# Hybrid decoder layer on one Trainium2 core: additions and low parts of the norms from GpSimd to VectorE, and the sample's retention matmuls placed later

## The chip, the cores and the metric

The kernel runs on one core of a Trainium2 chip. The metric is the time of one execution in microseconds, measured on the device. The kernel before takes 2187.86 us, the median of three runs (2186.29 to 2188.22).

## What is computed

One step of a decoder layer for two groups of requests that share the weights: a prompt of 1024 tokens and a sample of 8 single tokens with their caches, 1032 columns in all. D_MODEL is 1024 and D_FF 2816, ALPHA the fourth root of 2. Cut to what matters here:

```
def layer_norm(x, g, b):
    mu = x.mean(-1, keepdims=True)
    var = jnp.square(x - mu).mean(-1, keepdims=True)
    return (x - mu) * lax.rsqrt(var + LN_EPS) * g + b

h = layer_norm(ALPHA * h + 0.5 * swiglu(h, up1, down1))
h = layer_norm(ALPHA * h + merge_branches(attn, ret, ...) )
h = layer_norm(ALPHA * h + 0.5 * swiglu(h, up2, down2))

# retention of the sample, per head, one token per request:
s_new = gamma * s_old + k (outer) v
o     = q @ s_new
```

The outputs are the layer's rows for both groups, the last 128 keys and values, and the retention states.

## The kernel before

**Layout.** Activations stand transposed: features on the 128 partitions, tokens along the row. Feature group d (0 to 7) of the residual is `Y(d, ...)`, kept in the tiles `ya` (d below 4) and `yb`. All 1032 columns are worked in three chunks of 384, 384 and 264 (`CH`). Each large product is made of three in a reduced format: a value x is kept as a high part and a low part (x less the high part), and TensorE adds high by high, high by low and low by high. The activations' parts stand in tiles `T` (`HH` and `HL` in the code).

**Weights.** Each 128x512 block of weights comes from memory into `raw`, a ring of four, over SP's queue of DMAs (L470). ScalarE writes its high part `w_hi`; VectorE subtracts that from `raw` and writes `w_lo`. VectorE therefore has a steady stream of `w_lo` operations in its queue in all stages.

**Stages.** FFN 1, norm 1 (`ln` with `li` 0), the combined projection with banded attention and retention beside it, the two gated output products, norm 2 (`ln` with `li` 1 for chunks 0 and 1, `ln_last` for chunk 2), FFN 2, norm 3 (`ln3`), and the output.

**What sets the order.** All engines run their queues in order, and the program writes one stream by hand with the class `Emit`. It keeps an estimated clock of TensorE (`E.pe`, which grows with each matmul) and an estimated free time of ScalarE, VectorE and GpSimd (`E.eng`). The helpers `E.mm`, `E.tr`, `E.act`, `E.tt`, `E.stt`, `E.ts`, `E.dve` and `E.ptt` emit one instruction and return its estimated end; `E.tt` and `E.stt` go to VectorE, `E.ptt` to GpSimd. The side work (norms, attention, retention) is written as generators. `yield t` means that a generator is taken up again at the first gap between two groups of matmuls where `E.pe` has reached t. So an estimate decides which matmuls of the main stream stand ahead of a generator's next matmul, and a different estimate moves everything that is emitted after it. Since the helpers record every operation at their own line, all TensorE matmuls have line L99, transposes L107, ScalarE L117, VectorE L121 and GpSimd's `tensor_tensor` L137; `rsqrt` runs on GpSimd at L753. Rows are told apart by their tiles.

**Banks.** The results of the main stream's units rotate through four PSUM banks (`mb`); a unit needs the evacuation of the unit four before it. Side work takes other banks from a pool (`sbanks`; the profile shows them as `sb` or `mb`).

**Norm 1 and 2, `ln`.** With a bank of the mean, VectorE subtracts it from the eight feature groups, ScalarE squares each difference into `lQ` or `lsq`, and seven additions gather the squares in `lQ`. A matmul with `onesm` makes the variance of it (L99, `onesm,ln`), GpSimd the inverse root, and another matmul spreads it over the partitions. Then VectorE multiplies each group by that and the gain; ScalarE adds the bias and, in norm 1, writes the high part to `HH`; the low part goes to `HL`. Norm 1 does this for d in `POOLD` (1, 4, 6) with one more operation on ScalarE, which adds the bias in place, and a subtraction on GpSimd; for the others VectorE does it in one `scalar_tensor_tensor`. The sums of y that the mean is made of are GpSimd's work as well (tile `ln` from `ln` and `ya` or `yb`), outside the diff.

**Norm 3, `ln3`.** The columns are transposed to rows of tokens, copied to `zt` by ScalarE, and VectorE takes the statistics. For chunks 0 and 1, six pieces of 128x512 each are scaled by ScalarE, multiplied by the gain on VectorE, added to the bias on GpSimd and stored.

**The sample's retention, `sret_gen`.** Eight units: half a head's states each, in two buffers `Sb` that take turns. For a unit GpSimd scales the state by gamma, four operations of VectorE add the outer product (`Sb` from `vB,so,Sb`), and one matmul with 128x512 (L99, `Sb,so`) reads the new state. Behind the matmul, SP's queue gets the store of the state (L1329) and the fetch of the state two units later into the same buffer (L1308, L1309), so that fetch waits for the store. The weight loads that the main stream needs stand in the same queue behind them.

Of the kernel before, what the change touches and what calls it, by code (L numbers as in the profile page):

```python
# [15 lines left out]
ALU = mybir.AluOpType  # L16
# [35 lines left out]
FETCH = 2.0  # L52
QUEUE = 8.0
SHORT = 1.3
POOLD = (1, 4, 6)
AHEAD = 0.5


# [170 lines left out]
def build(tc, I, O):  # L229
    nc = tc.nc  # L230
    E = Emit(nc)
    ctx = ExitStack()
    with ctx:
# [310 lines left out]
        def ln(c, li, t):  # L544
            n0, N = CH[c]
            W = LNW[c]
            nb = N // W
            while lnlock[0] is not None:
                yield 0.0
            lnlock[0] = c  # L550
            S = env["lS"][c % 2]
            lQ, lsq = env["lQ"], env["lsq"]
            yield t
            b1 = yield from sbanks.get()
            E.mm(b1[:, :N], onesm, S[:, :N], True, True)
            ts_ = {}
            for d in range(KD + 2):
                if d < KD:
                    yd = Y(d, n0, n0 + N)
                    t1 = E.tt(yd, yd, b1[:, :N], ALU.subtract, n=N)  # L560
                    q = lQ if d == 0 else lsq[d % 3]
                    ts_[d] = E.act(q[:, :N], yd, AF.Square, n=N, after=t1)
                e = d - 2
                if e > 0:
                    q = lsq[e % 3]
                    t = (E.ptt if e % 2 else E.tt)(lQ[:, :N], lQ[:, :N], q[:, :N], ALU.add, n=N, after=ts_[e])
                if d % 2 and d < KD:
                    yield E.pace(AHEAD) if li else E.pe + 0.9
            sbanks.put(b1, t1)
            yield t + 2.0 * li  # L570
            b2 = yield from sbanks.get()
            for i in range(nb):
                E.mm(b2[:W, i * P:(i + 1) * P], lQ[:, i * W:(i + 1) * W], onesm, True, True)
            t = E.ts(lv[:W, 0, :nb], b2[:W, 0:nb * P:P], LN_EPS, ALU.add, n=3)
            sbanks.put(b2, t)
            yield rsqrt(lv[:W, 0, :nb], lv[:W, 1, :nb], t)
            b3 = yield from sbanks.get()
            for i in range(nb):
                E.mm(b3[:, i * W:(i + 1) * W], lv[:W, 1, i:i + 1].to_broadcast([W, P]), ident[:W, :W], True, True)
            ts_ = {}  # L580
            for d in range(KD + 2):
                if d < KD:
                    yd = Y(d, n0, n0 + N)
                    t1 = E.stt(yd, yd, lnp[:, 2 * li, d:d + 1], b3[:, :N], ALU.mult, ALU.mult, n=N)
                    bd = lnp[:, 2 * li + 1, d:d + 1]
                    if li == 1:
                        t = E.act(yd, yd, AF.Identity, bias=bd, n=N, ptr=1, after=t1)
                    else:
                        t = E.act(HH(d, n0, N), yd, AF.Identity, bias=bd, n=N, ptr=1, after=t1)
                        if d in POOLD:  # L590
                            t = E.act(yd, yd, AF.Identity, bias=bd, n=N, ptr=1, after=t1)
                    ts_[d] = t
                e = d - 2
                if e >= 0 and li == 0:
                    ye = Y(e, n0, n0 + N)
                    he, le = f(HH(e, n0, N)), HL(e, n0, N)
                    if e in POOLD:
                        E.ptt(le, ye, he, ALU.subtract, n=N, after=ts_[e])
                    else:
                        t = E.stt(le, ye, lnp[:, 2 * li + 1, e:e + 1], he, ALU.add, ALU.subtract, n=N, after=ts_[e])  # L600
                if d % 2 and d < KD - 1:
                    yield E.pace(AHEAD) if li else E.pe + 0.9
            if li == 1:
                ds(out=hres[:, :, n0:n0 + N], in_=env["ya"][:, :, n0:n0 + N])
            sbanks.put(b3, t1)
            lnlock[0] = None
# [53 lines left out]
        def ln3(c):  # L660
# [5 lines left out]
            lQ, lsq = env["lQ"], env["lsq"]  # L666
# [12 lines left out]
            for pi, ds_ in enumerate(pieces):  # L679
# [4 lines left out]
                n = len(ds_) * P  # L684
# [29 lines left out]
            def norm(k):  # L714
                return E.act(zs[k], zs[k], AF.Identity, scale=r[:, k // 2:k // 2 + 1], bias=nm[:, k // 2:k // 2 + 1], n=512, ptr=2)

            if not smp:
                yield t
                E.stt(nm, mv[:, :, 0], -1.0, r, ALU.mult, ALU.mult, n=3)
                for k in ks:  # L720
                    t = E.tt(zs[k], zs[k], Gs[k], ALU.mult, n=512, after=norm(k))
                    E.ptt(zs[k], zs[k], Bs[k], ALU.add, n=512, after=t)
                    out(k)
                    yield E.pe + 1.0
                return
# [574 lines left out]
        def sret_gen():  # L1300
# [12 lines left out]
            t = E.act(v32, b[:32, 0:P], n=128)  # L1313
# [5 lines left out]
            for u in range(2 * RH):  # L1319
                h, hf = u // 2, u % 2  # L1320
                S, V = Sb[u % 2], vB[u % 2]
                t = E.pscale(S, S, GAMMA[h], n=512)
                yield t
                for i in range(4):
                    t = E.stt(S[:, i, :], V[:, i, :], so[:, 0, h, 4 * hf + i:4 * hf + i + 1], S[:, i, :], ALU.mult, ALU.add, n=128)
                yield t
                b = yield from sbanks.get()
                E.mm(b[:8, :], so[:, 1, h, :], S.rearrange("p b e -> p (b e)"), True, True)
                ds(out=O["ss"][h, :, 4 * hf:4 * hf + 4, :], in_=S)  # L1329
                if u + 2 < 2 * RH:  # L1330
                    fetch(u + 2)
                for i in range(4):
                    ii = 4 * hf + i
                    src = b[:8, i * P:(i + 1) * P]
                    if ii == 0:
                        t = E.ts(o8, src, i8[:, ii:ii + 1], ALU.mult, n=128)
                    else:
                        t = E.stt(o8, src, i8[:, ii:ii + 1], o8, ALU.mult, ALU.add, n=190)
                sbanks.put(b, t)
                if not hf:  # L1340
                    yield E.pe + 2.0
                    continue
                E.dve("bn_stats", 128, out=bn8[:, 0:6], in_=o8)
                E.dve("bn_aggr", 13, out=bn8[:, 6:8], in_=bn8[:, 0:6])
                t = rsqrt(bn8[:, 8:9], bn8[:, 9:10], E.ts(bn8[:, 8:9], bn8[:, 7:8], GN_EPS, ALU.add, n=1))
                yield t
                t = E.ts(zp, o8, bn8[:, 6:7], ALU.subtract, bn8[:, 9:10], ALU.mult, n=128)
                yield t
                b = yield from sbanks.get()
                E.tr(b[:, 0:8], zp, ident[:8, :8])  # L1350
                t = E.stt(Y(4 + h, NP, T), b[:, 0:8], 0.5, so[:, 3, h, :], ALU.mult, ALU.mult, n=8)
                sbanks.put(b, t)
                yield E.pe + 2.0
# [631 lines left out]
```

## Time and profile before

| what | value |
|---|---|
| median of three runs | 2187.86 us |
| the profiled execution | 2186.94 us |
| its span | 2185.2 us |
| TensorE busy | 2124.8 us, 97% |
| VectorE busy | 1486.8 us, 68% |
| ScalarE busy | 836.4 us, 38% |
| GpSimd busy | 201.3 us, 9% |
| mean granted clock of TensorE | 0.992 |

Busy times are those of the engine's own instructions. PE is TensorE, PEld its weight loads, DVE VectorE, ACT ScalarE, POOL GpSimd, SP the engine that issues the DMAs. A row of a timeline gives the start in us from the span's start, the duration of the row, the engine and line, the operation, the tile that is written, the tiles that are read, and how many like instructions the row joins; in brackets stands the idle time of the engine ahead of it and what released it. A row of a table of stretches gives the length and then the busy time of each engine with its number of instructions, the granted clock, and the DMAs' share. All times come from one execution under the profiler.

### The profile page before, as it was taken

The numbers are of one execution on the slowest core, as the hardware profiler recorded it, in microseconds if no ns is written. First come the engines' busy times: TensorE is split into PE (matmuls) and PEld (weight loads), VectorE is DVE, ScalarE is ACT, GpSimd is POOL, SyncE is SP. The second block draws the span as 40 slices with busy tenths as digits, with TensorE's granted clock in tenths as the row PEclk, the third lists the DMA queues.
The fourth block names the chain that finished last, engine by engine and source line by source line (L and its number), as shares of the span: only waits on it lengthen the run. The fifth ranks groups of instructions, "written<-read, shape, count | busy, mean of one in ns | idle before, by whom it ended". The sixth has DMA issues, their size and how long they took to land.

```text
span 2185.2 us, 39568 instructions
## 1 busy us (share of the span) xinstructions
PE 2124.8 (97%) x15865; PEld 2089.1 (96%) x15865; DVE 1486.8 (68%) x2699; ACT 836.4 (38%) x1585; POOL 201.3 (9%) x235
## 2 busy tenths in 40 slices
PE   8999999999999999999999999998999999999996
PEld 8999999999999889999979999997999999999996
DVE  7766666676866885566666747787767666576757
ACT  5333333342433674111324434544333333342323
POOL 1000000000005343111110201010000000000004
PEclk9999999999999999999999999999999999999998
DMA  4333333272630120111253434531323323364332
GB/s 141 119 100 115 117 104 111 99 295 66 235 128 28 48 61 21 41 41 41 90 182 129 138 125 135 184 123 58 118 97 127 107 98 127 105 263 167 135 98 78
DMA packets 116314, 250.85 MB, mean 115 GB/s; under 512 B 14242, under 2 KB 18178, under 8 KB 112274
## 3 DMA queue, kind: packets, MB, share of 16 engines
q1 hardware_dynamic: 115778, 248.27, 32.8%
q8 instruction: 125, 2.05, 0.4%
q14 instruction: 59, 0.48, 0.1%
q0 software_dynamic: 352, 0.05, 0.1%
HBM read 195.01 MB, written 54.29 MB: 114 GB/s over the span
## 4 chain that ended last, share of the span: by engine, by line
PE 82%; DVE 9%; DMA 4%; ACT 2%; issue 2%; POOL 1%; SPq 0%; DVEq 0%; ACTq 0%; POOLq 0%
PE pr L99 54%; PE mb L99 26%; DMA raw<-in_w_dram 3%; PE sb L99 1%; DVE T L121 1%; DVE ya L121 1%; DVE yb L121 1%; DVE w_lo L121 1%; DVE ln L121 1%; DVE zt L121 1%; ACT w_hi L117 1%; DMA adr<-ya 1%; PE sb L107 1%; DVE st L121 0%; ACT T L117 0%
## 5 line engine op out<-in xcount | busy, mean ns | idle before, releaser
L99 PE MATMUL pr<-T,w_hi 128*128 128x258 f32 x7008 | 1139.5, 285 | 22.1 <-DVE yb L121 5.6
L99 PEld LDWEIGHTS pr<-T,w_hi 128*128 128x128 f32 x7008 | 973.8, 191 | 27.3 <-ACT w_hi L117 8.3
L99 PE MATMUL pr<-T,w_lo 128*128 128x258 f32 x3504 | 710.4, 284 | 1.0 <-DVE w_lo L121 1.0
L99 PEld LDWEIGHTS pr<-T,w_lo 128*128 128x128 f32 x3504 | 548.1, 191 | 1.4 <-DVE w_lo L121 1.4
L99 PE MATMUL mb<-T,w_hi 128*128 128x384 f32 (+1 forms) x2208 | 526.7, 325 | 1.8 <-DVE yb L121 1.8
L121 DVE TENSOR_TENSOR w_lo<-raw,w_hi 128x512 fp32r<-128x512 f32 x500 | 355.8, 730 | 128.8 <-ACT w_hi L117 127.9
L117 ACT ACTIVATE w_hi<-raw 128x512 fp32r<-128x512 f32 x500 | 304.7, 625 | 272.4 <-PE pr L99 147.1
L99 PEld LDWEIGHTS mb<-T,w_hi 128*128 128x128 f32 x2208 | 378.6, 189 | 9.3 <-issue 5.5
L99 PE MATMUL mb<-T,w_lo 128*128 128x384 f32 (+1 forms) x1104 | 353.7, 320 | 0.0
L99 PEld LDWEIGHTS mb<-T,w_lo 128*128 128x128 f32 x1104 | 207.9, 188 | 0.0
L117 ACT ACTIVATE w_hi<-st 128x512 fp32r<-128x512 f32 x174 | 108.3, 630 | 187.2 <-DVE st L121 103.6
L121 DVE TENSOR_TENSOR a<-pr,a 128x516 f32<-128x516 f32 x87 | 60.5, 696 | 89.1 <-PE pr L99 85.4
L121 DVE TENSOR_TENSOR w_lo<-st,w_hi 128x512 fp32r<-128x512 f32 x174 | 115.4, 683 | 5.0 <-ACT w_hi L117 5.0
L117 ACT ACTIVATE a<-pr 128x516 f32<-128x516 f32 x86 | 51.5, 600 | 100.1 <-PE pr L99 97.5
L121 DVE SCALAR_TENSOR_TENSOR yb<-pr,yb 128x516 f32<-128x516 f32 x72 | 49.9, 694 | 54.0 <-PE pr L99 54.0
L121 DVE SCALAR_TENSOR_TENSOR ya<-pr,ya 128x516 f32<-128x516 f32 x72 | 49.9, 693 | 54.0 <-PE pr L99 53.9
L137 POOL TENSOR_TENSOR ln<-ya 128x384 f32<-128x384 f32 (+1 forms) x6 | 6.8, 1127 | 776.2 <-DVE ya L121 776.1
L117 ACT ACTIVATE th<-a 128x516 f32<-128x516 f32 x43 | 27.3, 635 | 126.0 <-DVE a L121 126.0
L121 DVE TENSOR_TENSOR T<-T 128x1032 fp32r<-128x1032 f32 (+1 forms) x72 | 70.5, 986 | 0.3 <-ACT T L117 0.3
L117 ACT ACTIVATE T<-T 128x1032 fp32r<-128x1032 f32 (+1 forms) x72 | 59.6, 863 | 18.2 <-DMA T<-tdr 17.1
L753 POOL TENSOR_TENSOR ln<-ln,mhalf 128x3 f32<-128x3 f32 (+2 forms) x4 | 3.5, 870 | 675.1 <-DVE ln L121 675.1
L121 DVE SCALAR_TENSOR_TENSOR gt<-gt,mb 128x384 f32<-128x384 f32 (+1 forms) x48 | 24.4, 509 | 60.6 <-PE mb L99 58.9
(320 smaller groups left out, 2288.6 us busy)
## 6 DMA issues: line engine op xcount, KB each, us to landing
raw<-in_w_dram SPq DMA_DIRECT2D x500, 256.0 KB, 2.9
T<-tdr SPq DMA_DIRECT2D x20, 1032.0 KB, 11.3
tdr<-ya SPq DMA_DIRECT2D x72, 258.0 KB, 2.6
T<-tdr SPq DMA_DIRECT2D x8, 2064.0 KB, 11.4
tdr<-s SPq DMA_DIRECT2D x40, 258.0 KB, 2.4
tdr<-m SPq DMA_DIRECT2D x32, 258.0 KB, 2.5
T<-adr SPq DMA_DIRECT2D x16, 516.0 KB, 4.7
out_yp_dram<-zt SPq DMA_DIRECT2D x16, 256.0 KB, 2.0
```

Of the source, the lines that this page charges most:

```text
L99: self.nc.tensor.matmul(out=out, lhsT=lhsT, rhs=rhs, start=start, stop=stop, **kw)
L107: self.nc.tensor.transpose(out=out, in_=in_, identity=ident)
L117: self.nc.scalar.activation(out=out, in_=in_, func=func, scale=scale, **kw)
L121: getattr(self.nc.vector, fn)(**kw)
L137: self.nc.gpsimd.tensor_tensor(out=out, in0=a, in1=b, op=op)
L753: nc.gpsimd.tensor_tensor(out=r, in0=v, in1=mhalf[:v.shape[0], :n], op=ALU.pow)
```

## The change

There are four edits:

1. `POOLD` is empty: in norm 1 the low parts of d 1, 4 and 6 go to VectorE in the one operation that the other groups use. Nine operations leave GpSimd (six of 384 columns, three of 264), nine leave ScalarE, nine are added to VectorE.
2. In `ln`, every addition of squares is VectorE's; four of seven in each chunk were GpSimd's. That is 12 in norm 1 and 8 in norm 2.
3. In `ln3`, the additions of the bias for chunks 0 and 1 are VectorE's (12 of 128x512). One in chunk 2 stays on GpSimd.
4. In `sret_gen`, the generator is taken up 2.5 us later, by the estimated clock, ahead of the matmul on `Sb`, and so are the store and the fetch behind it. This applies to all eight units.

```diff
--- before.py
+++ after.py
@@ -52,7 +52,7 @@
 FETCH = 2.0
 QUEUE = 8.0
 SHORT = 1.3
-POOLD = (1, 4, 6)
+POOLD = ()
 AHEAD = 0.5
 
 
@@ -563,7 +563,7 @@
                 e = d - 2
                 if e > 0:
                     q = lsq[e % 3]
-                    t = (E.ptt if e % 2 else E.tt)(lQ[:, :N], lQ[:, :N], q[:, :N], ALU.add, n=N, after=ts_[e])
+                    t = E.tt(lQ[:, :N], lQ[:, :N], q[:, :N], ALU.add, n=N, after=ts_[e])
                 if d % 2 and d < KD:
                     yield E.pace(AHEAD) if li else E.pe + 0.9
             sbanks.put(b1, t1)
@@ -718,8 +718,8 @@
                 yield t
                 E.stt(nm, mv[:, :, 0], -1.0, r, ALU.mult, ALU.mult, n=3)
                 for k in ks:
-                    t = E.tt(zs[k], zs[k], Gs[k], ALU.mult, n=512, after=norm(k))
-                    E.ptt(zs[k], zs[k], Bs[k], ALU.add, n=512, after=t)
+                    E.tt(zs[k], zs[k], Gs[k], ALU.mult, n=512, after=norm(k))
+                    E.tt(zs[k], zs[k], Bs[k], ALU.add, n=512)
                     out(k)
                     yield E.pe + 1.0
                 return
@@ -1323,7 +1323,7 @@
                 yield t
                 for i in range(4):
                     t = E.stt(S[:, i, :], V[:, i, :], so[:, 0, h, 4 * hf + i:4 * hf + i + 1], S[:, i, :], ALU.mult, ALU.add, n=128)
-                yield t
+                yield t + 2.5
                 b = yield from sbanks.get()
                 E.mm(b[:8, :], so[:, 1, h, :], S.rearrange("p b e -> p (b e)"), True, True)
                 ds(out=O["ss"][h, :, 4 * hf:4 * hf + 4, :], in_=S)
```

TensorE has the same 7240 rows of program as before, and SP the same 762; VectorE has 2408 in place of 2383, GpSimd 168 in place of 196 and ScalarE 1322 in place of 1335 (a row joins like instructions).

Here is VectorE in norm 1, the first chunk, where the subtractions of the mean (`ya,sb` and `yb,sb`) and the additions of squares (`ln<-ln`) stand among the evacuations of the last units of FFN 1 (`ya` or `yb` from `mb`); a minus is a row that stood there before, a plus one that stands there now.

```order
 L121 SCALAR_TENSOR_TENSOR ya<-mb_6807,ya 128x384
 L121 TENSOR_TENSOR ya<-ya,sb_97 128x384 x4
+L121 TENSOR_TENSOR ln<-ln 128x384
 L121 SCALAR_TENSOR_TENSOR ya<-mb_6808,ya 128x384
 L121 TENSOR_TENSOR yb<-yb,sb_97 128x384
 L121 TENSOR_TENSOR ln<-ln 128x384
-L121 TENSOR_TENSOR yb<-yb,sb_97 128x384 x2
+L121 TENSOR_TENSOR yb<-yb,sb_97 128x384
 L121 TENSOR_TENSOR ln<-ln 128x384
 L121 TENSOR_TENSOR yb<-yb,sb_97 128x384
+L121 TENSOR_TENSOR ln<-ln 128x384
+L121 TENSOR_TENSOR yb<-yb,sb_97 128x384
```

The additions that GpSimd did now stand between the subtractions, so the later subtractions and the evacuations behind them have more rows ahead of them.

The next rows are TensorE's in the sample's retention, before the change, around the matmul of the fourth unit (`Sb,so`); the other rows are a unit of the combined projection, one row of high parts and one of low parts for each half of a k-tile pair (`T`).

```order
L99 MATMUL mb_6805<-T_146,w_hi_70 128x384 x2
L99 MATMUL mb_6805<-T_146,w_lo_78 128x384
L99 MATMUL mb_6805<-T_146,w_hi_70 128x384 x2
L99 MATMUL mb_6805<-T_146,w_lo_78 128x384
L99 MATMUL sb_96<-Sb_10711,so 8x512
L99 MATMUL mb_6805<-T_147,w_hi_65 128x384 x2
L99 MATMUL mb_6805<-T_147,w_lo_73 128x384
```

The same place after the change:

```order
L99 MATMUL mb_6805<-T_146,w_hi_72 128x384 x2
L99 MATMUL mb_6805<-T_146,w_lo_80 128x384
L99 MATMUL mb_6805<-T_147,w_hi_69 128x384 x2
L99 MATMUL mb_6805<-T_147,w_lo_77 128x384
L99 MATMUL mb_6805<-T_147,w_hi_69 128x384 x2
L99 MATMUL mb_6805<-T_147,w_lo_77 128x384
L99 MATMUL mb_6810<-Sb_10702,so 8x512
L99 MATMUL mb_6805<-T_148,w_hi_69 128x384 x2
L99 MATMUL mb_6805<-T_148,w_lo_77 128x384
```

The matmul on `Sb` stood after the rows of `T_146`, with those of `T_147` and `T_148` behind it. It now stands after those of `T_147`: two more k-tiles of the unit are ahead of it.

The last place is VectorE around the update of `Sb` for the same unit, before:

```order
L121 TENSOR_TENSOR w_lo_75<-raw_82,w_hi_67 128x512
L121 SCALAR_TENSOR_TENSOR yb<-mb_6810,so 128x8
L121 SCALAR_TENSOR_TENSOR Sb_10710<-vB_10712,so,Sb_10710 128x128 x4
L121 SCALAR_TENSOR_TENSOR gt_10707<-gt_10707,mb_6807 128x384
L121 TENSOR_TENSOR w_lo_76<-raw_83,w_hi_68 128x512
L121 TENSOR_TENSOR w_lo_79<-raw_84,w_hi_71 128x512
L121 TENSOR_SCALAR o_10714<-mb_6809,i_93 8x128
L121 SCALAR_TENSOR_TENSOR o_10714<-mb_6809,i_93,o_10714 8x128 x3
L121 SCALAR_TENSOR_TENSOR gt_10708<-gt_10708,mb_6808 128x384
L121 TENSOR_TENSOR gt_10707<-gt_10707,gt_10708 128x384
L121 SCALAR_TENSOR_TENSOR Sb_10711<-vB_10713,so,Sb_10711 128x128 x4
L121 SCALAR_TENSOR_TENSOR g_lo<-gt_10707,g_hi 128x384
```

And after:

```order
L121 SCALAR_TENSOR_TENSOR Sb_10701<-vB_10703,so,Sb_10701 128x128 x4
L121 TENSOR_TENSOR w_lo_78<-raw_83,w_hi_70 128x512
L121 TENSOR_TENSOR w_lo_73<-raw_84,w_hi_65 128x512
L121 TENSOR_SCALAR o_10705<-mb_6809,i_93 8x128
L121 SCALAR_TENSOR_TENSOR o_10705<-mb_6809,i_93,o_10705 8x128 x3
L121 TENSOR_TENSOR w_lo_74<-raw_81,w_hi_66 128x512
L121 TENSOR_TENSOR w_lo_75<-raw_82,w_hi_67 128x512
L121 SCALAR_TENSOR_TENSOR gt_10698<-gt_10698,mb_6807 128x384
L121 SCALAR_TENSOR_TENSOR Sb_10702<-vB_10704,so,Sb_10702 128x128 x4
L121 SCALAR_TENSOR_TENSOR gt_10699<-gt_10699,mb_6808 128x384
L121 TENSOR_TENSOR gt_10698<-gt_10698,gt_10699 128x384
L121 SCALAR_TENSOR_TENSOR g_lo<-gt_10698,g_hi 128x384
```

Before, the update stood behind the pair `w_lo_76` and `w_lo_79`, four operations on `o` and two on the gate. Now it stands ahead of that pair, right behind the pair of `w_lo_74` and `w_lo_75`, and the operations on `o` of the unit before it have moved up as well.

## The prediction

> **What bounds the kernel now.** I read the page first, then the waits of TensorE, then a table of stretches, and last the rows of the stretches that the change touches. The page says who the limit is.
>
> ```profile
> span 2185.2 us, 39568 instructions
> PE 2124.8 (97%) x15865; PEld 2089.1 (96%) x15865; DVE 1486.8 (68%) x2699; ACT 836.4 (38%) x1585; POOL 201.3 (9%) x235
> ```
>
> TensorE is busy for 97% of the span, and the change removes none of its instructions. So the change can only work on the 60.4 us in which TensorE idles. The profiled execution took 2186.94 us, which is its span and 1.74 us around it, and 0.92 below the median of 2187.86. I make the sum against 2186.94 and add 0.92 at the end. The next view lists what those idle times waited for (total, times, longest).
>
> ```profile
> PE sb L99 <- DVE Sb L121: 3.9, 2, 2.9
> PE sb L99 <- POOL ln L137: 3.6, 3, 1.3
> ...
> PE mb L99 <- DVE Sb L121: 3.0, 2, 2.7
> ...
> PE mb L99 <- POOL ln L137: 2.0, 1, 2.0
> ```
>
> Two causes belong to the change: waits for GpSimd's additions in a norm (3.6 + 2.0) and for VectorE's update of the sample's retention state `Sb` (3.9 + 3.0). The table of stretches shows where the idle time is, and how full VectorE is there.
>
> ```profile
> core 0: us, PE busy (x) PEld busy (x) DVE busy (x) ACT busy (x) POOL busy (x), PEclk, DMA share, GB/s
> ...
> 680.00:720.00 40.00, 35.60 (x227) 33.96 (x226) 34.43 (x58) 18.27 (x35) 23.86 (x29) 0.96 0.24 69
> 720.00:800.00 80.00, 75.03 (x465) 68.02 (x464) 65.18 (x213) 57.26 (x181) 29.83 (x37) 1.00 0.13 41
> ...
> 1080.00:1160.00 80.00, 73.12 (x370) 62.10 (x369) 51.63 (x131) 23.14 (x45) 8.82 (x12) 0.98 0.55 177
> ...
> 1370.00:1380.00 10.00, 9.05 (x76) 8.84 (x75) 9.19 (x18) 6.29 (x14) 3.19 (x3) 1.00 0.47 141
> ...
> 2140.00:2186.00 46.00, 28.30 (x199) 26.98 (x197) 34.32 (x63) 14.52 (x24) 21.03 (x16) 0.84 0.25 93
> ```
>
> TensorE idles 4.4 and 5.0 us around the first norm, 6.9 in the sample's retention, 0.95 at the second norm and 17.7 in the tail. VectorE has 5.6 us free of 40 at the first norm, the fullest stretch of these, so what it takes over from GpSimd there is not free.
>
> **Part 1 and 2, the first norm.** Each of three chunks waits for the last addition of squares before its variance matmul; a fourth wait is for a `yb` evacuation.
>
> ```profile
> 684.18 0.94 PE L99 MATMUL sb<-onesm,ln 128*128 128x128 f32 x6 [1.29 <-POOL ln L137]
> ...
> 698.40 0.51 PE L99 MATMUL mb<-T,w_hi 128*128 128x264 f32 x2 [1.80 <-DVE yb L121]
> ...
> 714.78 0.94 PE L99 MATMUL sb<-onesm,ln 128*128 128x128 f32 x6 [1.31 <-POOL ln L137]
> ...
> 734.71 0.89 PE L99 MATMUL mb<-onesm,ln 128*88 128x128 f32 x6 [2.04 <-POOL ln L137]
> ```
>
> The rows that price an operation on either engine (VectorE, then GpSimd; start, duration, count, wait):
>
> ```profile
> 674.53 1.95 DVE L121 TENSOR_TENSOR ya<-ya,sb 128x384 f32<-128x384 f32 x4
> ...
> 677.57 1.13 DVE L121 TENSOR_TENSOR ln<-ln 128x384 f32<-128x384 f32 x1
> ...
> 679.89 0.56 DVE L121 TENSOR_TENSOR ln<-ln 128x384 f32<-128x384 f32 x1 [0.26 <-POOL ln L137]
> ...
> 689.63 0.61 DVE L121 SCALAR_TENSOR_TENSOR T<-ya,lnp,T 128x384 fp32r<-128x384 f32 x1
> ...
> 712.64 2.64 DVE L121 TENSOR_TENSOR w_lo<-raw,w_hi 128x512 fp32r<-128x512 f32 x2
> ...
> 726.95 1.44 DVE L121 TENSOR_TENSOR ya<-ya,mb 128x264 f32<-128x264 f32 x4
> ```
> ```profile
> 683.14 0.99 POOL L137 TENSOR_TENSOR ln<-ln 128x384 f32<-128x384 f32 x1 [0.56 <-DVE ln L121]
> ...
> 713.29 1.44 POOL L137 TENSOR_TENSOR ln<-ln 128x384 f32<-128x384 f32 x1
> ```
>
> Four subtractions take 1.95, so 0.49 each at 384 columns and 0.36 (1.44 / 4) at 264. An addition of squares takes 0.56 alone and 1.13 while GpSimd runs; GpSimd needs 0.99 for one, and 1.44 where VectorE competes with it. Chunk 0: 8 subtractions, 7 additions and 3 evacuations (as the order has them), 18 x 0.49 = 8.8 from 674.53, end at 683.3; GpSimd still sums the rows of y, and one more blocked addition (0.57) makes 683.6 at the middle, against 683.14 + 0.99 = 684.13 now: 0.6 of the 1.29 goes. Chunk 1: GpSimd's last addition ended at 713.29 + 1.44 = 714.73. On VectorE it no longer lies beside the two `w_lo` of 712.64; put ahead of them, with the three other additions (1.5) less the two blocked ones that become short (1.1), it ends near 713.7: 1.0 of 1.31. Chunk 2: 15 x 0.36 = 5.4 from 726.95 ends at 732.4, and TensorE arrives at 734.71 - 2.04 = 732.67: all 2.04 go. Together 3.6.
>
> Against it stands VectorE's added work: 8 additions of 0.49, 4 of 0.36, six low parts of 0.53 and three of 0.39 (the 0.61 row less what overlaps its neighbour, scaled for 264), 9.7 us in all. The low parts stand ahead of evacuations for which TensorE's next units wait, so I keep the 1.80 wait and take 0.6 off: **-3.0**. Bounds: nothing gained (VectorE as late as GpSimd was), and all four waits gone, -6.4. The nine removed copies on ScalarE cost nothing either way: its busy time in 680 to 720 is 18.3 of 40.
>
> **Part 4, the sample's retention.** The waits for `Sb` sum to 6.9 us (the list above), four in all, each before the second matmul of a pair; the two long ones, and VectorE before the first of them, stand in these rows.
>
> ```profile
> 1116.59 1.86 PE L99 MATMUL sb<-Sb,so 128*8 128x512 f32 x2 [2.90 <-DVE Sb L121]
> ...
> 1151.62 1.02 PE L99 MATMUL mb<-Sb,so 128*8 128x512 f32 x2 [2.69 <-DVE Sb L121]
> ```
> ```profile
> 1112.28 0.69 DVE L121 TENSOR_TENSOR w_lo<-raw,w_hi 128x512 fp32r<-128x512 f32 x1 [1.95 <-ACT w_hi L117]
> ...
> 1115.31 1.14 DVE L121 SCALAR_TENSOR_TENSOR Sb<-vB,so,Sb 128x128 f32<-128x128 f32 x4
> ```
>
> The update of `Sb` at 1115.31 is late because VectorE, in order, stood at a `w_lo` that waited 1.95 us for its `w_hi`, whose raw weights came behind two stores and two refetches of `Sb` in SP's queue. The edit lets 2.5 us of other matmuls through first: in the order the second unit's matmul now has six k-tiles of a projection unit ahead of it instead of four. It leaves 0.40 of 2.90 and 0.19 of 2.69, and nothing of the two short ones (6.9 - 2.90 - 2.69 = 1.3): -6.3. The store and refetch behind each matmul move too, past weight loads in SP's queue; the order shows the pairs of stores spread apart, with four weight loads between, which should help the late `w_hi`. But a first unit's update now stands behind a later pair of `w_lo`, and for that I allow +1.0: **-5.3**. Bounds: -6.9 (all waits gone), and a loss of 2.0, if one late raw load (the 1.95) now also holds a unit that did not wait. The evacuations of gates behind the moved matmuls are covered by four rotating banks; if that cover fails, the price is a wait as long as a gate's evacuation, inside the same bounds.
>
> **Part 2 in the second norm.** The same move of additions meets 0.95 us of TensorE's idle time in 1370 to 1380. VectorE is busy 9.19 of 10 there, so **-0.7**, between 0 and -0.95.
>
> **Part 3, the tail.** The stretch that counts runs on VectorE from the second chunk's scaling to the reduction that the last group of matmuls needs (rows of VectorE, then one of GpSimd).
>
> ```profile
> 2157.46 0.69 DVE L121 TENSOR_TENSOR zt<-zt,gb 128x512 f32<-128x512 f32 x1 [0.94 <-ACT zt L117]
> ...
> 2158.41 1.66 DVE L121 TENSOR_TENSOR zt<-zt,gb 128x512 f32<-128x512 f32 x1
> ...
> 2164.88 0.69 DVE L121 TENSOR_TENSOR zt<-zt,gb 128x512 f32<-128x512 f32 x1 [1.36 <-ACT zt L117]
> ...
> 2169.63 0.69 DVE L121 TENSOR_TENSOR zt<-zt,gb 128x512 f32<-128x512 f32 x1 [1.15 <-ACT zt L117]
> ...
> 2170.58 1.12 DVE L121 COPY ln<-ya 128x32 f32<-128x32 f32 x1
> 2171.62 0.17 DVE L121 COPY ln<-yb 128x32 f32<-128x32 f32 x1
> 2171.82 0.27 DVE L121 TENSOR_REDUCE ln<-ln 128x8 f32<-128x64 f32 x1
> ```
> ```profile
> 2158.23 1.29 POOL L137 TENSOR_TENSOR zt<-zt,gb 128x512 f32<-128x512 f32 x1 [1.99 <-DVE zt L121]
> ```
>
> It lasts 2171.82 - 2157.46 = 14.4 us. Of the six multiplications three are of the 0.69 form (0.61 less its overlap with the next, so far as VectorE is alone) and three of the 1.66 form (1.57 so), because GpSimd's addition of 1.29 runs beside them: 6.5. Two waits for ScalarE's `zt` are 1.36 + 1.15 = 2.5. A copy of 32 columns takes 1.12 beside GpSimd, 0.17 alone. The rest, evacuations and statistics, is 14.4 - 6.5 - 2.5 - 1.3 = 4.1. Then: 12 operations of 0.61, 7.3; the rest 4.1; two copies 0.3; and one of the two waits, 1.3, since VectorE now comes later to ScalarE's results: 13.0, so **-1.4**. Bounds: both waits stay (0), or neither (-2.6). In the first chunk four operations now stand between two evacuations where two multiplications stood, 4 x 0.61 = 2.4 for about 2 x 1.57 = 3.1; no evacuation comes later there than by one such operation, and the four banks that rotate hide it; uncovered it would cost that 0.6.
>
> The Trainium skill (SBUF — State Buffer, Who interferes with whom) says that a VectorE operation with two SBUF inputs contends with GpSimd's reads, and that the holder of the shared pair fully blocks the other. By that rule a multiplication beside an addition would last up to 0.61 + 1.29 = 1.90; the row has 1.66, so the trace bears out contention, but not quite a wait for the whole instruction. With 1.90 in place of 1.66 the three pairs would give back 0.7 us more: -2.1 for the tail.
>
> **Sum.** -3.0 - 5.3 - 0.7 - 1.4 = -10.4: 2176.5 for an execution like the profiled one, 2177.5 against the median.
>
> **The rivals.**
> VectorE gains nothing at the first norm (B): its 9.7 us of new work use up what the waits give back, since only 5.6 us are free in 680 to 720. For it speaks that stretch, against it that blocked additions become short (1.13 to 0.56). It gives 2177.5 + 3.0 = 2180.5.
>
> The retention's waits only move (E): the change does not do what it says, because the delay also puts off the refetch, and VectorE's update stays as late against TensorE as it was. For it: the update waits for weights, not for TensorE; against it: 2.5 us of matmuls are available, and the first matmul of each pair never waited. It gives 2177.5 + 5.3 = 2182.8.
>
> VectorE becomes the bound at the first norm (C, the other side). The low parts and additions stand ahead of evacuations of `mb` banks, four matmul groups fill the four banks, and TensorE stops until VectorE has caught up. It decides once the backlog exceeds the free 5.6 us together with the relief from blocking, some five additions of 0.57, 2.9 in all, in that stretch. Then the added 9.7 passes to TensorE in place of the gain: 2177.5 + 3.0 + 9.7 = 2190.2, and 2191.9 to 2193.6 if one or two more waits cost 1.7 us of clock each, as below. For it: the 1.80 wait for `yb` already is of this kind; against it: about half of the added work falls into 720 to 800, where 14.8 us are free.
>
> Waits cost clock as well (D). The granted clock after three waits:
>
> ```profile
> 700.00:702.00 2.00, 2.00 (x8) 1.39 (x7) 2.00 (x6) 0.63 (x1) 1.84 (x3) 0.50 0.38 124
> 702.00:704.00 2.00, 2.00 (x13) 2.00 (x13) 1.94 (x5) 0.94 (x2) 0.66 (x1) 0.66 0.43 142
> ...
> 1118.00:1120.00 2.00, 2.00 (x7) 1.61 (x6) 1.36 (x5) 0.00 (x0) 0.00 (x0) 0.55 0.70 242
> 1152.00:1154.00 2.00, 2.00 (x10) 1.44 (x9) 1.22 (x4) 0.01 (x1) 0.00 (x0) 1.00 0.35 131
> ```
>
> After the 1.80 wait the clock was 0.50 and 0.66 (4 us, 1.7 lost); after the 2.90 wait 0.55 (0.9 lost in 2 us); after the 2.69 wait full. If shorter waits take both dips away, 1.7 + 0.9 = 2.6 us come on top: 2174.9. The Trainium skill (TensorE: Matmul & The Clock Gate, HAM oscillation) asks for no idle gap over some 3.4 us. By that rule none of these waits could cost clock and D would bring nothing; the rows at 0.50 to 0.66 behind 1.80, and 0.55 behind 2.90, disagree, the full clock behind 2.69 does not.
>
> **How the numbers follow.** Forecast 0.45, B 0.18, E 0.15, D 0.10, C 0.12. The likeliest gives the time, 2177.5. All good bounds together are -6.4 - 6.9 - 0.95 - 2.6 = -16.9 (2171.0), all bad ones +2.0 (2189.9); 8 in 10 reaches from 2172, D with some terms at their good ends, to 2186, past E with part of its terms at their bad ends, and leaves out C. A measurement of this kernel can tell about 0.2%, 4.4 us: faster is under 2183.5, slower over 2192.2. Faster: 0.43 of the forecast, 0.15 of B, 0.07 of E and 0.09 of D, 0.74. Slower: 0.06 of C and 0.02 for the rest, 0.08. Same: 0.18.
>
> **What would show it.** Right: the waits of TensorE have no row for GpSimd's `ln` at L137, and 1.5 us or less for `Sb`; TensorE idles under 7 us in 680 to 800 and under 2.5 us in the 80 us of the sample's retention; additions of squares last 0.56, not 1.1; the tail's reduction starts 13 us after the second chunk's first multiplication. Wrong: waits for VectorE's `ya`, `yb` or `ln` at the first norm that sum to what GpSimd's did (B) or to over 10 us (C); four waits for `Sb` of the old length (E); no half-clock slices at either place and a gain over 12 (D). A new wait over 2 us outside these places would mean that the reordered attention or loads cost something that no term here has.

## The result: 2174.17 us, and the profile after

The changed kernel takes 2174.17 us (median of four runs, 2173.55 to 2176.21) against 2187.07 (four runs): ratio 0.9937, 95% interval 0.9925 to 0.9948, or 12.9 us less by the medians. The forecast was 10.4 us less, 2177.5. The time lies in the range that was given (2172 to 2186), but the interval of the gain, 11.4 to 16.4 us, leaves 10.4 out: the change brought more than was forecast.

The page's first lines, and those of TensorE's waits after the change that answer to the ones shown before:

```profile
span 2171.7 us, 39563 instructions
...
PE 2118.9 (98%) x15865; PEld 2084.4 (96%) x15865; DVE 1493.9 (69%) x2740; ACT 832.6 (38%) x1576; POOL 154.2 (7%) x194
```
```profile
PE mb L99 <- DVE ln L121: 7.3, 3, 5.0
...
PE sb L99 <- DVE ln L121: 2.8, 2, 1.7
...
PE mb L99 <- POOL ln L137: 0.5, 1, 0.5
```

No row for `Sb` is left, and GpSimd's `ln` has fallen from 5.6 us to 0.5 (a wait for the sums of y). In its place stand 3.4 us for VectorE's `ln` at norm 1: the 2.8, and 0.6 of the 7.3. The span is 13.5 us shorter, of which TensorE's idle time is 7.6 (60.4 to 52.8) and its busy time 5.9 (2124.8 to 2118.9). TensorE runs the same instructions, so most of the shorter busy time is a higher clock: summed over stretches of 2 us, the busy time lost to a lowered clock is 10.5 us before and 6.2 after. The other 1.6 us have no explanation here. The stretches show where (of the changed kernel, then the tail of the kernel before with the same length):

```profile
680.00:720.00 40.00, 36.10 (x237) 34.45 (x236) 36.53 (x68) 17.04 (x32) 14.74 (x21) 1.00 0.15 44
720.00:800.00 80.00, 75.83 (x471) 69.33 (x470) 70.90 (x237) 57.37 (x183) 20.27 (x27) 1.00 0.16 53
1080.00:1160.00 80.00, 80.00 (x430) 72.50 (x428) 53.93 (x124) 27.28 (x54) 8.44 (x11) 1.00 0.55 181
1370.00:1380.00 10.00, 9.84 (x81) 9.85 (x82) 9.05 (x17) 7.81 (x17) 0.10 (x1) 1.00 0.59 187
2098.50:2171.70 73.20, 57.13 (x381) 55.96 (x379) 49.64 (x103) 21.43 (x35) 4.73 (x5) 0.90 0.16 59
```
```profile
2112.00:2185.20 73.20, 56.30 (x372) 54.92 (x370) 47.75 (x90) 20.69 (x33) 22.16 (x17) 0.90 0.16 59
```

Idle time fell by 0.5 and 0.8 us at norm 1 (4.4 to 3.9, 5.0 to 4.2), by 6.9 in the sample's retention, where none is left, by 0.8 at norm 2 and by 0.8 in the tail. The granted clock rose from 0.96 to 1.00 in 680 to 720 and from 0.98 to 1.00 in the retention. About 1.9 us of idle time came back in the first 40 us, which no edit touches. There the execution of before is the unusual one: TensorE is busy for 33.8 to 34.5 us of these 40 in eleven of the fourteen profiles, and for 35.6 to 36.0 in three, before among them.

Norm 1's matmuls in the changed kernel, with VectorE's last additions ahead of them:

```profile
685.87 0.94 PE L99 MATMUL sb<-onesm,ln 128*128 128x128 f32 x6 [1.09 <-DVE ln L121]
...
701.55 0.51 PE L99 MATMUL mb<-T,w_hi 128*128 128x264 f32 x2 [0.49 <-DVE ya L121]
...
714.67 0.94 PE L99 MATMUL sb<-onesm,ln 128*128 128x128 f32 x6 [1.73 <-DVE ln L121]
...
735.85 0.89 PE L99 MATMUL mb<-onesm,ln 128*88 128x128 f32 x6 [0.58 <-DVE ln L121]
```
```profile
684.00 1.81 DVE L121 TENSOR_TENSOR ln<-ln 128x384 f32<-128x384 f32 x2
...
694.30 0.60 DVE L121 SCALAR_TENSOR_TENSOR T<-ya,lnp,T 128x384 fp32r<-128x384 f32 x1
...
713.05 1.56 DVE L121 TENSOR_TENSOR ln<-ln 128x384 f32<-128x384 f32 x2
...
734.28 1.51 DVE L121 TENSOR_TENSOR ln<-ln 128x264 f32<-128x264 f32 x3
```

The variance matmul still waits in each chunk, now for VectorE's own additions (1.09, 1.73, 0.58). The 1.80 us wait for `yb` is down to 0.49 for `ya`. A low part takes 0.60 with nothing on GpSimd beside it.

SP's queue in the sample's retention, before and after:

```profile
1095.23 0.38 SPq L1329 DMA_DIRECT2D out_ss_dram<-Sb  x1
1098.91 0.33 SPq L1308 DMA_DIRECT2D Sb<-in_st_dram  x1
...
1099.80 0.38 SPq L1329 DMA_DIRECT2D out_ss_dram<-Sb  x1
1103.81 0.33 SPq L1308 DMA_DIRECT2D Sb<-in_st_dram  x1
...
1104.71 8.62 SPq L470 DMA_DIRECT2D raw<-in_w_dram  x6
```
```profile
1097.72 0.33 SPq L1308 DMA_DIRECT2D Sb<-in_st_dram  x1
...
1098.61 2.35 SPq L470 DMA_DIRECT2D raw<-in_w_dram  x4
1101.01 0.42 SPq L1329 DMA_DIRECT2D out_ss_dram<-Sb  x1
1106.53 0.33 SPq L1308 DMA_DIRECT2D Sb<-in_st_dram  x1
...
1107.44 7.59 SPq L470 DMA_DIRECT2D raw<-in_w_dram  x6
```

Before, two fetches of `Sb` (1098.91 and 1103.81) each stood about 4 us behind a store, and no load of weights went out from 1095.23 to 1104.71. After, four loads go out between two such pairs; each fetch still stands behind its store, the second by 5.5 us.

### The profile page after: what moved, and what is told of

It is laid out like the page before. It is cut to its first block, busy times and chain, and to the rows that moved or that the text cites. A ratio compares the mean times of both kernels' runs of the same rounds, so it can differ in the third digit from the quotient of the medians.

```text
span 2171.7 us, 39563 instructions
## 1 busy us (share of the span) xinstructions
PE 2118.9 (98%) x15865; PEld 2084.4 (96%) x15865; DVE 1493.9 (69%) x2740; ACT 832.6 (38%) x1576; POOL 154.2 (7%) x194
## 4 chain that ended last, share of the span: by engine, by line
PE 85%; DVE 9%; DMA 2%; issue 2%; ACT 1%; POOL 1%; SPq 0%; DVEq 0%; ACTq 0%; POOLq 0%
PE pr L99 55%; PE mb L99 27%; DMA raw<-in_w_dram 2%; PE sb L99 2%; DVE ya L121 2%; DVE T L121 1%; DVE w_lo L121 1%; DVE yb L121 1%; DVE ln L121 1%; DVE zt L121 1%; PE sb L107 1%; PE mb L107 0%; DVE st L121 0%; POOL pt L137 0%; DMA ya<-in_x_dram 0%
## 5 line engine op out<-in xcount | busy, mean ns | idle before, releaser
L121 DVE TENSOR_TENSOR ln<-pr,ln 128x516 f32<-128x516 f32 x43 | 29.9, 695 | 49.5 <-PE pr L99 49.5
L99 PE MATMUL mb<-o_hi,w_hi 128*128 128x384 f32 (+1 forms) x192 | 62.0, 323 | 0.0
L99 PE MATMUL mb<-g_lo,w_hi 128*128 128x384 f32 (+1 forms) x192 | 61.6, 321 | 0.0
## 6 DMA issues: line engine op xcount, KB each, us to landing
T<-tdr SPq DMA_DIRECT2D x20, 1032.0 KB, 11.2
T<-tdr SPq DMA_DIRECT2D x8, 2064.0 KB, 11.4
```

The source lines that it names most:

```text
L99: self.nc.tensor.matmul(out=out, lhsT=lhsT, rhs=rhs, start=start, stop=stop, **kw)
L121: getattr(self.nc.vector, fn)(**kw)
```

## Experiments

All ratios are against the kernel before on the same chip. "Clock loss" is the mean over a kernel's runs of span times one less the granted clock; "at full clock" is span times clock, less that of the kernel before. The clock loss also counts half clock (a stretch with a granted clock of about 0.5) while TensorE idles, which costs nothing (6.8 of 17.3 us in the profile of before, nearly all in the tail), so only its differences are read.

| kernel | runs | ratio (95%) | us off, by ratio | clock loss, us (before) | at full clock, us |
|---|---|---|---|---|---|
| retention alone | 11 | 0.9976 (0.9966 to 0.9986) | 5.3 | 17.5 (18.3) | -5.2 |
| norms alone | 7 | 0.9973 (0.9962 to 0.9985) | 5.9 | 16.2 (18.3) | -5.1 |
| four buffers | 11 | 0.9977 (0.9967 to 0.9987) | 5.0 | 16.9 (18.3) | -3.9 |
| transfers late | 8 | 0.9968 (0.9956 to 0.9980) | 7.0 | 16.1 (18.3) | -5.8 |
| additions alone | 11 | 0.9982 (0.9972 to 0.9992) | 3.9 | 14.9 (18.6) | -1.0 |
| low parts alone | 11 | 0.9978 (0.9968 to 0.9988) | 4.8 | 15.7 (18.6) | -1.7 |
| tail alone | 12 | 0.9998 (0.9989 to 1.0007) | 0.4 | 18.8 (18.6) | -1.1 |
| changed kernel again | 5 | 0.9936 (0.9924 to 0.9948) | 14.0 | 14.3 (18.6) | -10.2 |
| sums too (a wrong result, see there) | 12 | 0.9979 (0.9970 to 0.9988) | 4.6 | 16.9 (18.7) | -3.3 |
| variance later | 8 | 0.9962 (0.9949 to 0.9975) | 8.3 | 18.5 (18.7) | -8.2 |
| additions back | 5 | 0.9935 (0.9922 to 0.9949) | 14.2 | 13.9 (19.9) | -8.1 |

The standard error of a clock loss is 0.5 to 1.5 us, that of a full-clock time 0.2 to 0.8. The chip's medians of the kernel before were 2188.41 (first four kernels), 2187.82 (next four), 2189.50 and 2189.80.

**Retention alone.** The fourth edit by itself:

```diff
-                yield t
+                yield t + 2.5
                 b = yield from sbanks.get()
                 E.mm(b[:8, :], so[:, 1, h, :], ...)
```

> Only the 2.5 us in the sample's retention; the norms as before. Theory M (the moved matmul covers VectorE's late update of Sb): the waits for Sb (6.9 us before) go, and the half-clock slice behind the 2.90 us wait (about 1.7 us) goes too, so 7 to 8.6 us off the kernel before, about 2179. Theory E (the waits only move, the gain came from the norms): within 1 us of before.

2183.21 us. The list of TensorE's waits has no `Sb` left, as theory M expected, but the time fell by 5.3 (3.1 to 7.4) and not by 7 to 8.6. Theory E is out.

**Norms alone.** The other three edits, without that one.

> The three edits in the norms; the sample's retention as before. Theory M: the idle time that went at norm 1 (1.3), norm 2 (0.5) and in the tail (1.3 to 2.1), 3 to 4 us off, up to 5.6 if the half clock behind norm 1's old 1.80 us wait stays away: about 2182.5. Theory E: nearly the whole gain, 12 us off. Rival C (VectorE is the bound at norm 1): no gain or slower than before.

2181.63 us, 5.9 off, just over what theory M allowed (5.6). Waits for `Sb` of 6.1 us remain:

```profile
PE sb L99 <- DVE Sb L121: 3.8, 2, 2.1
...
PE mb L99 <- DVE Sb L121: 2.3, 3, 0.9
```

**Four buffers.** The kernel before, its order unchanged; two more buffers for the state lie in the part of tile `ln` that no norm uses at that time.

```diff
-                ds(out=Sb[u % 2], in_=I["st"][h, :, 4 * hf:4 * hf + 4, :])
+                ds(out=Sb[u % 4], in_=I["st"][h, :, 4 * hf:4 * hf + 4, :])
...
-                S, V = Sb[u % 2], vB[u % 2]
+                S, V = Sb[u % 4], vB[u % 2]
```

> The kernel before, order unchanged, but the retention state of the sample takes turns in four buffers and not two, so that no fetch in SP's queue waits for a store. Theory Q (the weights behind those fetches come late, and VectorE with them): the waits for Sb go without any later matmul, 6 to 8 us off. Theory M alone (the matmul is simply too close behind its update): the waits for Sb stay at about 6.9 and the time within 1 us of before.

2183.64 us. The waits for `Sb` fell from 6.9 to 1.4 with not one matmul moved:

```profile
PE sb L99 <- DVE Sb L121: 1.1, 1, 1.1
...
PE mb L99 <- DVE Sb L121: 0.3, 1, 0.3
```

In its queue the fetches go out right behind the stores (stores at 1101.41 and 1104.51, fetches at 1101.89 and 1104.91). So the cause of most of these waits was the fetch that stood behind a store in SP's queue and held the weight loads, as theory Q has it. The matmul's nearness to its update was not enough to make them. The time fell by 5.0 (2.8 to 7.2), somewhat less than the 6 to 8 of theory Q.

**Transfers late.** The matmul behind its update as before; the store, the fetch and what follows 2.5 us later.

```diff
                 E.mm(b[:8, :], so[:, 1, h, :], ...)
-                ds(out=O["ss"][h, :, 4 * hf:4 * hf + 4, :], in_=S)
-                if u + 2 < 2 * RH:
-                    fetch(u + 2)
...
                 sbanks.put(b, t)
+                yield E.pe + 2.5
+                ds(out=O["ss"][h, :, 4 * hf:4 * hf + 4, :], in_=S)
+                if u + 2 < 2 * RH:
+                    fetch(u + 2)
```

> The matmul on Sb where it stood, right behind its update; only the store, the fetch and what follows come 2.5 us later, so that SP's queue has the order of the changed kernel (weight loads between the two stores). Theory Q: the weights come in time, the waits for Sb are gone or under 2 us in all, 5 to 8 us off. Theory M: VectorE's update ends where it did against TensorE, so waits of 5 us or more remain, and the gain is under 2 us.

2180.50 us, 7.0 off, as much as the edit itself within the intervals.

```profile
PE mb L99 <- DVE Sb L121: 0.7, 1, 0.7
...
PE sb L99 <- DVE Sb L121: 0.6, 2, 0.3
```

Waits of 1.3 us remain. Theory Q holds again: the later place of the transfers does nearly all, the later matmul the last 1.3.

**Additions alone** (the second edit).

> Only the additions of squares go to VectorE (norms 1 and 2); low parts, tail and retention as before. Theory P (the waits are GpSimd's, 5.6 us in the list, and VectorE's own additions give some of them back): 1.5 to 3.5 us off in TensorE's idle time, the waits for GpSimd's ln gone. Rival C: VectorE is late by as much, 0 or slower. Clock slices can add or take 1.7 each.

2184.31 us, 3.9 off; but only about 1.0 of it at full clock, and 3.7 in the clock. The waits for GpSimd's `ln` went from 5.6 to 0.7, but the gain at full clock is short of the 1.5 to 3.5 of theory P.

**Low parts alone** (the first edit).

> Only the nine low parts of norm 1 go to VectorE. Theory P: VectorE gets 4.5 us of work beside its evacuations and no wait for GpSimd goes, so 0 to 1.5 us slower, with a longer wait for yb or ya near 700. Rival: since the low parts on GpSimd block VectorE's own (1.31 instead of 0.61), they are free on VectorE and 0 to 1.5 us come off.

2183.91 us, 4.8 off, more than either expectation. Norm 1 in this kernel:

```profile
698.19 0.51 PE L99 MATMUL mb<-T,w_hi 128*128 128x264 f32 x2 [1.48 <-DVE yb L121]
...
714.43 0.94 PE L99 MATMUL sb<-onesm,ln 128*128 128x128 f32 x6 [2.76 <-POOL ln L137]
```

The wait for `yb` got shorter (1.80 to 1.48) although VectorE had more to do. The table has 1.7 us at full clock and 2.9 in the clock. The 2.76 was 1.31 before; why it could grow stands below, under norm 1.

**Tail alone** (the third edit).

> Only the additions of norm 3 for the first two chunks go to VectorE. Theory P: the stretch from the second chunk's first multiplication to the reduction goes from 14.4 to about 13.3 us, as in the changed kernel, and 1.1 to 2.1 us come off the time; rival: ScalarE is the limit there, and under 0.3 comes off.

2187.24 us; the interval allows 2.0 us faster to 1.5 slower. The stretch went from 14.4 to 13.3 us (2161.34 to 2174.63), as in the changed kernel, whose first and last rows of it stand below. By the time alone this edit's effect stays open; at full clock it is 1.1 us, with a standard error of 0.5.

```profile
2145.01 1.42 DVE L121 TENSOR_TENSOR zt<-zt,gb 128x512 f32<-128x512 f32 x2 [0.94 <-ACT zt L117]
...
2158.30 0.27 DVE L121 TENSOR_REDUCE ln<-ln 128x8 f32<-128x64 f32 x1
```

**The changed kernel again.**

> The changed kernel once more, beside the parts and on the same chip. Theory S (the parts add up: 5.2 for the retention alone and 6 to 7 for the norms alone): ratio 0.9937 to 0.9950, 11 to 14 us off. If the parts stood in each other's way, clearly less than 11; if the clock carried a share of its own, its granted clock stays at 0.993 to 0.994 against 0.992 before.

2174.31 us. 5.3 and 5.9 for its two halves make 11.2; the whole has 14.0, between 11.4 and 16.6, so the halves do not stand in each other's way.

**Additions back.** The changed kernel with the second edit undone.

> The changed kernel with the additions of squares back on GpSimd in turn; low parts, tail and retention as in the change. Theory S (the parts add up; the additions alone gave 4.0): 9 to 11 us off the kernel before, ratio 0.9950 to 0.9960, and waits for GpSimd's ln of 4 to 5 us in the list again. Theory O (additions and low parts take the same waits and the same half-clock slice away, so one of them is nearly enough): within 2 us of the changed kernel, ratio 0.9935 to 0.9946.

2176.27 us, and a ratio of 0.9935 beside 0.9936 for the whole change. Its waits for GpSimd's `ln` are back:

```profile
PE sb L99 <- POOL ln L137: 4.9, 3, 2.7
```

By the ratio theory O holds: beside the other edits the additions bring nothing that these runs can tell from zero. At full clock it has 8.1 against 10.2, which would be some 2 us for the additions; the ratio's interval (0.9922 to 0.9949) does not exclude that.

**Sums too.** The changed kernel with the sums of y moved from GpSimd to VectorE as well.

```diff
-                return E.ptt(S, Y(0, n0, n0 + N), Y(1, n0, n0 + N), ALU.add, n=N, after=t)
+                return E.tt(S, Y(0, n0, n0 + N), Y(1, n0, n0 + N), ALU.add, n=N, after=t)
             elif d > 1:
-                return E.ptt(S, S, Y(d, n0, n0 + N), ALU.add, n=N, after=t)
+                return E.tt(S, S, Y(d, n0, n0 + N), ALU.add, n=N, after=t)
```

> The changed kernel with the sums of y for the norms on VectorE too, so that GpSimd has no addition left in norms 1 and 2. Theory P (VectorE still has room at norm 1: 36.5 of 40 busy in 680 to 720): 21 more operations of 0.36 to 0.49 cost within 2 us of the changed kernel, about 2174 to 2176. Rival C (it becomes the bound there): waits for evacuations of yb and ya over 3 us in 690 to 720, and 2178 or more.

2183.47 us, some 9 slower than the changed kernel by the ratios. This kernel's first output is wrong, by a relative error of 0.068, and why is not known. So it is no kernel to use, and it only shows the time of these instructions in this order. TensorE now waits for VectorE in many small pieces:

```profile
PE mb L99 <- DVE T L121: 3.5, 5, 1.9
...
PE mb L99 <- DVE ya L121: 3.3, 2, 1.7
...
PE mb L99 <- DVE w_lo L121: 1.6, 1, 1.6
```

This is rival C, one step further than the change goes.

**Variance later.** The changed kernel with norm 1's variance matmul taken up 1.5 us later.

```diff
-            yield t + 2.0 * li
+            yield t + (2.0 if li else 1.5)
```

> The changed kernel with norm 1's variance matmul taken up 1.5 us later, the retention's cure applied to the waits that norm 1 has left (1.1 + 1.7 + 0.6 for ln). Theory P (these waits are of the same kind): 2 to 3.4 us less, about 2171 to 2172. Rival: what follows the variance in the chain comes later by as much, and the waits move to the projection's first matmuls: within 1 us of the changed kernel, or slower.

2180.22 us, about 6 slower than the changed kernel. The waits for `ln` went, and three for the inverse root came in their place:

```profile
PE mb L99 <- POOL lv L753: 5.7, 3, 4.0
```
```profile
744.00:748.00 4.00, 1.70 (x8) 1.70 (x9) 3.11 (x13) 0.00 (x0) 0.85 (x1) 0.55 0.01 2
748.00:752.00 4.00, 4.00 (x18) 4.00 (x17) 2.82 (x7) 2.61 (x7) 1.93 (x3) 0.60 0.00 0
```

A 3.95 us wait in 742 to 746 is followed by the clock at 0.55 and 0.60. The norm is a chain; the retention's matmul was not on one.

**Gaps.** The kernel before with 20 gaps put into FFN 1.

```diff
+                E.mm(b[:, 0:P], onesm, onesm, True, True)
+                t = E.act(x, b[:, 0:P], n=P)
+                for _ in range((0, 2, 5, 8, 12)[i % 5]):
+                    t = E.act(x, x, n=P)
+                E.mm(b[:, P:2 * P], onesm, x, True, True)
```

> The kernel before with 20 idle gaps of TensorE put into FFN 1, 26 us apart, four each of five lengths (about 0.6 to 4 us): a small matmul, a chain of 1, 3, 6, 9 or 13 copies on ScalarE, a matmul that needs their result. Theory D (waits well under 3.4 us cost clock too, by chance, so that each us of wait costs over 1 us): half-clock slices behind some of the gaps of 1.5 to 3 us, and the time grows by more than the gaps' sum. Rival (only gaps over some 3.4 us do; the dips of the other traces have another cause): half clock behind the four longest alone, and the others cost their length or less.

2268.56 us, ratio 1.0368 (1.0351 to 1.0385), 79.1 us more. The gaps' waits and TensorE's busy time in this kernel:

```profile
PE sb L99 <- ACT so L117: 46.8, 20, 5.4
```
```profile
PE 2155.1 (95%) x15945; PEld 2117.1 (93%) x15945; DVE 1486.0 (66%) x2699; ACT 874.6 (39%) x1713; POOL 200.7 (9%) x235
```

The gaps sum to 46.8 us. The busy time is 30.3 us longer than before (2155.1 against 2124.8); the 40 small matmuls take 11.9 of it, and the other 18.4 are the old matmuls, slower at a lower clock: 0.4 us for each us of gap. (The clock loss rose by 27.8, from 18.7 to 46.5, but part of that is half clock inside the gaps, where nothing runs.) Four of the gaps, and the clock behind them:

```profile
140.08 0.49 PE L99 MATMUL sb<-so,onesm 128*128 128x128 f32 x2 [1.05 <-ACT so L117]
...
168.37 0.49 PE L99 MATMUL sb<-so,onesm 128*128 128x128 f32 x2 [2.24 <-ACT so L117]
...
198.28 0.80 PE L99 MATMUL sb<-so,onesm 128*128 128x128 f32 x2 [3.09 <-ACT so L117]
...
469.81 0.49 PE L99 MATMUL sb<-so,onesm 128*128 128x128 f32 x2 [2.07 <-ACT so L117]
```
```profile
140.00:144.00 4.00, 3.92 (x32) 3.92 (x33) 1.29 (x2) 0.67 (x2) 0.00 (x0) 1.00 0.11 43
168.00:172.00 4.00, 3.63 (x30) 3.63 (x31) 1.62 (x3) 1.58 (x3) 0.00 (x0) 1.00 0.20 70
...
198.00:200.00 2.00, 1.72 (x8) 1.72 (x9) 0.00 (x0) 0.23 (x1) 0.00 (x0) 0.50 0.00 0
...
470.00:472.00 2.00, 2.00 (x12) 2.00 (x12) 0.00 (x0) 0.00 (x0) 0.00 (x0) 0.61 0.03 8
472.00:474.00 2.00, 2.00 (x12) 2.00 (x11) 0.70 (x1) 0.53 (x1) 0.00 (x0) 0.54 0.00 0
```

Eight gaps of 0.37 to 1.05 us left the clock alone. Of three of 2.07 to 2.24, one was followed by half clock (470) and two were not (168, 617). All five of 3.04 to 3.16 and all four of 4.46 to 5.42 were. So theory D is right for some of the waits of about 2 us and for all from 3.04 us on, and the rival's border lies lower than it said.

## Why the prediction was right, and where it was not

- **Where the time comes from.** The idle time that the terms name fell by 1.3 + 6.9 + 0.8 + 0.8 = 9.8 us in the profile, and by 10.2 at full clock over the runs of the changed kernel again; forecast were 10.4. That 9.8 lies so near is in part luck: norm 1 gave 1.7 less idle time than forecast and the retention 1.6 more. Measured in time, from the last matmul of FFN 1 that writes `pr` to the first of FFN 2 that does, the stretch went from 801.9 us (654.65 to 1456.51) to 790.3 (656.53 to 1446.79), and from the last such matmul of FFN 2 to the end from 71.8 to 70.8: 12.6 together, of 13.5 in the span. The same middle stretch took 805.9 and 806.0 in two kernels that do not change it (gaps, tail alone), so one profile is uncertain by some us there.
- **Norm 1, -3.0.** 1.3 was measured as idle time. The step that failed is how the waits go: 0.6 of 1.29 (0.5 by its own figures, 684.13 - 683.6), 1.0 of 1.31 and "all 2.04 go" were forecast, and the 1.80 kept; 1.29, 1.31 and 2.04 became 1.09, 1.73 and 0.58, and the 1.80 became 0.49. In the first chunk VectorE's last two additions take 1.81 together, beside a sum of y on GpSimd, and end hardly sooner than GpSimd's did. The second chunk is another matter. Its variance matmul starts 28.8 us after the first chunk's and no longer 30.6 (714.67 - 685.87, 714.78 - 684.18), so the additions are done sooner. Its wait grew all the same, because before, the half clock in 700 to 704 had held TensorE back, and so hid a part of the wait. In three kernels that keep norm 1 as it was, but whose profile has the full clock in 700 to 704 or its like (tail alone, four buffers, gaps), this wait is 2.7 to 2.8. Busy time times granted clock in 680 to 800 rose by 2.7 us (36.10 + 75.83 against 35.60 x 0.96 + 75.03), so the -3.0 is about right in size, with half of it from the clock. The low parts were costed at a loss of 0.6, which the runs do not bear out: alone they took 4.8 us off. The 1.80 wait that the prediction kept for them was the one that got shorter.
- **The sample's retention, -5.3.** The profile shows -6.9 of idle time, the edit alone 5.3 by time. The step "the edit lets 2.5 us of other matmuls through first", which leaves 0.40 and 0.19, names the smaller cause. Four buffers with no matmul moved took 5.5 of the 6.9 away, and late transfers with the matmul at its update 5.6. What the prediction told in passing, the stores spread apart with loads between, is the main cause. The +1.0 for updates behind later `w_lo` pairs was not needed.
- **Norm 2, -0.7.** 0.8.
- **The tail, -1.4.** The stretch on VectorE is 13.3 us instead of 13.0, TensorE's idle time 0.8 less. One of the two waits for ScalarE stayed (1.03), as assumed.
- **The clock.** This is what the sum left out, and the step that failed most: the clock's term was put at nothing in the forecast and went to rival D, with a chance of 0.10 and a price of 2.6. The runs show a clock loss of 14.1 to 14.3 us with the change and 18.3 to 19.9 before, some 4 us. What the prediction named as D's sign, no half-clock slice at the two places and a gain over 12, came true, so D describes the result better than the forecast does. Its price was a little small: behind the 2.90 wait, 1116 to 1118 is at 0.59 as well as 1118 to 1120 at 0.55, so the two places cost 1.7 and 1.5 us of busy time.
- **Where half clock stands.** The other profiles bear this out. All six kernels whose waits for `Sb` sum to 5.5 us or more have one stretch of half clock in the retention (at 1116 before, 1148 norms alone, 1102 additions alone, 1146 low parts alone, 1156 tail alone, 1218 gaps), and none of the eight with 1.4 us or less has one there. But not each wait has its half-clock slice: four waits had one together, and an unchanged wait of 2.2 us at 46 us was followed by half clock in nine of the fourteen profiles, not in that of the kernel before, but in that of the changed kernel:

```profile
40.00:56.00 16.00, 13.82 (x115) 13.60 (x114) 14.34 (x16) 8.94 (x13) 0.00 (x0) 1.00 0.15 46
```
```profile
40.00:56.00 16.00, 13.80 (x102) 13.59 (x101) 13.85 (x16) 9.05 (x13) 0.00 (x0) 0.89 0.14 44
```

So the price is one of chance: 46.8 us of gaps, most of them over 2 us, made the other matmuls 18.4 us slower. The change took out three waits over 2 us (2.04, 2.90, 2.69) and one of 1.80. The Trainium skill (TensorE: Matmul & The Clock Gate, HAM oscillation) puts the border at gaps over some 3.4 us. The traces agree for the four gaps of 4.46 to 5.42, each followed by half clock, but here 3.04 to 3.16 were so five times in five and 2.07 to 2.24 once in three.
- **Rival B** is half right: VectorE's own additions now make the waits at norm 1, but they sum to 3.4 us where GpSimd's summed to 4.6, and the clock adds to the gain. **Rival E** is out by the run with that edit alone. **Rival C** did not come with this change, and did with 21 more operations on VectorE.
- **The signs.** Those for a right forecast held for `Sb`, the retention and the tail, but TensorE idles 8.1 us in 680 to 800, not under 7, and GpSimd's `ln` keeps a row of 0.5.
- **Contention.** The multiplications and additions in the tail last 0.7 each (1.42 for two) and no longer 1.66, and a low part at norm 1 0.60, as the rows of before promised for VectorE alone. The prediction read the 1.66 as less than a wait for the whole addition on GpSimd. By its rows that addition ends at 2159.52 (2158.23 + 1.29) and the multiplication at 2160.07, 0.55 later, which is about its time alone; so the rows do fit a wait for the whole of what was left of the addition.

What stays open: how much of the gain belongs to the additions beside the low parts (0 to 2 us), whether the tail's edit shows in the time at all, and why the low parts alone lower the clock loss as much as they seem to (2.9 us, with an error near 1.0). A hint for the last is that the 1.80 wait was followed by half clock in three of six profiles, and the 1.48 that low parts on VectorE leave in neither of two; that is too few to settle it. Nor are waits the only cause of half clock: in three profiles (retention alone, transfers late, sums too) it stands near 850, behind sixteen matmuls of 8 columns and no wait.

## What to carry to other kernels

Where an engine waits for an operation that is late, look for what holds the operation in the queues ahead of it, DMA queues too: here it was a fetch behind a store with weight loads behind both, and either spacing them or giving the fetch another buffer took most of the wait away. Waits of about 2 us and more on TensorE can cost more than their length, 1.4 us for each us in the run with gaps, so an edit that removes such waits should be priced above their sum. Moving work to a busier engine pays while that engine has room, and 21 operations further the same move lost 9 us.

## What was not expected of the hardware

Half clock followed idle gaps of TensorE from about 2 us on (in the kernel itself from 1.80), by chance, and from 3.04 us on in all nine gaps tried; none followed the eight of 1.05 us or less. Half clock behind one wait also shortens the next, since TensorE arrives later: 1.31 us in place of 2.7 to 2.8 at norm 1. The clock loss of one and the same kernel varies from run to run and makes most of its spread: the 29 runs of the kernel before on one chip have a standard error of 0.5 us in time and of 0.2 in span times clock.
